# Dilated attention computed on even and odd tokens apart, and the next layer's first weight tile split on GpSimd alone

## The chip, the cores and the metric

The kernel runs on one core of a Trainium2 chip. The metric is device time in microseconds (us) of one execution; less is better. The core's engines are TensorE (PE in the rows, its weight loads PEld), VectorE (DVE), ScalarE (ACT), GpSimd (POOL) and SyncE (SP), which here only issues the DMAs.

## The reference

A decoder trunk of two layers over 256 tokens of width 1024, in float32. Each layer has a gated token mixer (short convolution, RWKV-7 and dilated attention in parallel) and then a mixture of 16 experts, of which each token uses two. The change touches the attention and the seam between the layers. Cut to what matters:

```python
DILATED_GROUPS = ((128, 1), (512, 4), (2048, 16))     # (window, dilation), 8 heads of 64 each
def dilated_attention_branch(z, cos, sin):            # SEQ = 256
    q, k, v = (...)                                   # (B, S, group, head, 64)
    q = apply_partial_rotary(q, cos, sin); k = apply_partial_rotary(k, cos, sin)
    for g, (window, dilation) in enumerate(DILATED_GROUPS):
        # query t attends keys t, t-d, t-2d, ..., t-window
        o, l = dilated_window_attention(q[:, :, g], k[:, :, g], v[:, :, g], window, dilation)
        outs.append(o); lses.append(l)
    wts = jax.nn.softmax(jnp.stack(lses, axis=0), axis=0)
    return sum over g of wts[g] * outs[g]
```

In the groups with dilation 4 and 16 an even token attends only even tokens and an odd token only odd ones.

## The kernel before

**Dense work.** Every dense product of the mixer runs as three fp32r matmuls (`mm3`, lines 405 to 407): input and weight are each split into a rounded part (`hi`) and the rest (`lo`), and hi*hi, hi*lo and lo*hi are added in PSUM. A weight tile of 128x1024 comes by DMA (`load`, line 350, issued by SP), is cast to `wh` on ACT (line 329) and subtracted to `wl` on DVE (line 330), both in `hilo`. `dense_w` makes channels by tokens (weights stationary, 256 tokens moving), `dense_t` tokens by channels (the input `xh`, `xl` stationary, 128 tokens at a time). `dense_t` is used for the attention's values and for the last projection.

**Chains.** The attention and the RWKV waves are generators. After every four contraction steps of dense work `pump` lets each live generator go one `yield` further, so their small matmuls stand between the dense ones in PE's queue. `STAGES` gives the order of the dense work in each layer, `LAG` adds empty steps to the generators. PE takes its queue in order.

**Attention.** For each layer, each half of the heads (`hh`, four heads) and each group `g` there is one generator, 12 in all, 8 of them with `g` = 1 or 2. It rotates q and k (lines 879 to 883); makes the scores in two query blocks, the first against 128 keys, the second against 256 (line 900); adds the mask (904); takes maxima (909); exponentiates (927); transposes the three 128x128 blocks of four heads each (939); copies them (941); multiplies by the values (952), with three blocks again; and merges the group into a running `acc`, with its denominators `den` and shifts `nm` (968 to 978).

**Experts.** In `moe` eight pairs of experts are done in turn: gate and up products (`gu`, line 1444), the activation (`th`, 1457 to 1459), its transpose (`ht`, 1472), the copy `hT` on ACT (1474), the down product (`db`, 1495), its scaled split `yh` on ACT (1499) and `yl` on DVE (1500), and the return to the tokens (`acc`, 1392). Their weights, 100 MB a layer, are used once and come through SP's queue in the order of use.

**The seam.** In the last pair of experts, before the last down matmuls, `split_ahead(nc.gpsimd, 1)` (line 1493) splits the first weight tile of the next layer (`wh`<-`raw`, from `in_wl`): the cast on ACT, the subtraction on POOL. After the last layer there is nothing to split. The order within each engine's queue is set by the scheduler of the framework, not by the text alone.

Of the kernel before, what the change touches and what calls it, by code (L numbers as in the profile page):

```python
# [12 lines left out]
ALU = mybir.AluOpType  # L13
# [4 lines left out]
S = 256  # L18
# [21 lines left out]
def _constants():  # L40

    p = np.arange(128)
    t = np.arange(64)
    out = {}
    out["ident"] = np.eye(128)
    scanm = np.ones((128, 512))
    scanm[:, ::64] = 0.0
    out["scanm"] = scanm
    s = (p % 64)[:, None]
    strict = (s < t[None]).astype(np.float64)  # L50
    incl = (s <= t[None]).astype(np.float64)
# [12 lines left out]
    for window, d in GROUPS:  # L64
        i = (128 + p)[:, None]
        j = np.arange(256)[None]
        ok = (j <= i) & ((i - j) % d == 0) & (i - j <= window)
        am.append(np.where(ok, 0.0, NEG))
    out["amask"] = np.concatenate(am, axis=1)
    out["place"] = np.broadcast_to(t[None] - FAR, (128, 64))  # L70
    inv = np.float32(500000.0) ** (-np.arange(0, 16, 2, dtype=np.float32) / np.float32(16))

    rot = np.zeros((4, 32))
    rot[0::2, :8] = -inv
    rot[1::2, :8] = inv
    out["invf"] = rot.reshape(128, 1)

    out["before"] = np.broadcast_to(np.where(np.tril(np.ones((4, 4)), -1), -1e-37, 0.0).reshape(1, 16), (128, 16))
    mixer = ("scanm", "zmask", "lev", "eye32", "blk", "amask")
# [145 lines left out]
class Net:  # L225
# [98 lines left out]
                                             src[i][:, (2 * pr + cc) * 128:(2 * pr + cc) * 128 + 128], self.c("ident"))  # L324
            yield pr, ps.rearrange("p (c t) -> p c t", c=2)

    def hilo(self, hi, lo, src, eng=None):

        r = self.nc.scalar.copy(hi, src)  # L329
        (eng or self.nc.vector).tensor_tensor(lo, src, hi.bitcast(F32), op=ALU.subtract)  # L330
        return r

# [48 lines left out]
        p = self.tc.tile_pool(name=name, bufs=1)  # L381
        return p, p.__enter__()

    def split_ahead(self, eng=None, n=SPLIT + 1):

        r = []
        i = self.asked
        while i < len(self.plan) and not self.plan[i][2]:
            i += 1
        while len(self.pre) < n and i + len(self.pre) < len(self.plan) and self.plan[i + len(self.pre)][2]:  # L390
            w = self.raw(i + len(self.pre))
            hi = self.t4(w.shape, "wh", F32R)
            lo = self.t4(w.shape, "wl", F32R)
            r.append(self.hilo(hi, lo, w, eng))
            self.pre.append((hi, lo))
        return r

# [27 lines left out]
                    self.pump()  # L425
        return ps

    def dense_t(self, x):

        xh, xl = x  # L430
        ps = [self.bank("dt") for _ in range(2)]
        for hf in range(2):
            wh, wl = self.next_parts()
            for i in range(2):
                t = slice(128 * i, 128 * i + 128)
                for kk in range(4):
# [430 lines left out]

    def attention(self, l, hh, g, q, k, v, st, yc):

        nc = self.nc  # L870
        for _ in range(LAG[l][6]):
            yield
        T = []
        for t, name in ((q, "qT"), (k, "kT")):
            tmp = self.t2([128, 2, S], "rt")
            for o in range(4):

                d, e = slice(32 * o, 32 * o + 32), slice(32 * (o ^ 1), 32 * (o ^ 1) + 32)
                nc.scalar.copy(tmp[d], t[e])
                yield  # L880
            nc.vector.tensor_tensor(tmp, tmp, self.sin.unsqueeze(1).to_broadcast([128, 2, S]), op=ALU.mult)
            nc.vector.tensor_tensor(t, t, self.cos.unsqueeze(1).to_broadcast([128, 2, S]), op=ALU.mult)
            nc.vector.tensor_tensor(t, t, tmp, op=ALU.add)
            T.append(t)
            yield
        for _ in range(LAG[l][7]):
            yield
        qT, kT = T
        s0 = self.t2([128, 2, 2, 128], "s0")
        s1 = self.t4([128, 2, 2, 256], "s1")  # L890
        mx = self.sm([128, 2, 2, 2], "mx")
        am = self.c("amask")
        for qb in range(2):
            nk = 128 * (qb + 1)
            s = (s0, s1)[qb]
            b = [self.bank("sc") for _ in range(2)]
            for hp in range(2):
                for e in range(2):
                    he = slice(64 * e, 64 * e + 64)
                    nc.tensor.matmul(b[e][:, hp * nk:hp * nk + nk], qT[he, hp, qb * 128:qb * 128 + 128], kT[he, hp, 0:nk], start=True, stop=True)  # L900
            yield
            o = g * 256 + 128 - qb * 128
            for e in range(2):
                nc.vector.tensor_tensor(s[:, e, :, :], b[e][:, 0:2 * nk].rearrange("p (h t) -> p h t", h=2),
                                        am[:, o:o + nk].unsqueeze(1).to_broadcast([128, 2, nk]), op=ALU.add)
                if e == 0:
                    yield
            yield
            nc.vector.tensor_reduce(mx[:, qb].rearrange("p hp e -> p e hp"), s, axis=AX.X, op=ALU.max)
        for _ in range(LAG[l][8]):  # L910
            yield
        nm = self.sm([128, 8], "nmx")
        m8 = mx.rearrange("p a b c -> p (a b c)")
        nc.vector.tensor_scalar(nm, m8, -0.125, None, op0=ALU.mult)
        if g:
            acc, den0, nm0 = st[-1]
            nc.vector.tensor_tensor(nm, nm0, nm, op=ALU.min)
            al = self.sm([128, 8], "al")
            nc.vector.tensor_tensor(al, nm, nm0, op=ALU.subtract)
            nc.scalar.activation(al, al, AF.Exp)  # L920
        den = self.sm([128, 8], "den")
        for qb in range(2):
            s = (s0, s1)[qb]
            for hp in range(2):
# [6 lines left out]
        pts = []  # L931
        for qb in range(2):
            s = (s0, s1)[qb]
            for kb in range(qb + 1):
                b = self.bank("pt")
                for hp in range(2):
                    for e in range(2):
                        o = (hp * 2 + e) * 128
                        nc.tensor.transpose(b[:, o:o + 128], s[:, e, hp, kb * 128:kb * 128 + 128], self.c("ident"))
                t = self.t2([128, 4, 128], "PT")  # L940
                nc.scalar.copy(t.rearrange("p a b -> p (a b)"), b)
                pts.append(t)
                yield
# [2 lines left out]
        o = self.bank("o")  # L946
        for qb in range(2):
            for hp in range(2):
                for kb in range(qb + 1):
                    for e in range(2):  # L950
                        h = 2 * hp + e
                        nc.tensor.matmul(o[64 * e:64 * e + 64, hp * 256 + qb * 128:hp * 256 + qb * 128 + 128], v[:, kb, h * 64:h * 64 + 64],
                                         pts[qb + kb][:, h, :], start=(kb == 0), stop=(kb == qb))
        yield
        t = self.t2([128, 2, 256], "oc")
        nc.scalar.copy(t.rearrange("p a b -> p (a b)"), o)
        yield
        o = self.bank("o")
        for qb in range(2):
# [18 lines left out]
            st.append((acc, den, nm))  # L978
        yield
        if g == 2:  # L980
            acc, dn, _ = st[-1]
            rd = self.sm([128, 8], "rd")
            nc.vector.reciprocal(rd, dn)
            nc.vector.tensor_tensor(acc, acc, bc(rd), op=ALU.mult)
# [7 lines left out]
                                        acc[:, i * 4 + cc * 2:i * 4 + cc * 2 + 2, :].rearrange("p h t -> p (h t)"), self.c("ident"))  # L992
            yield
            hi, lo = yc
            bv = b.rearrange("p (c t) -> p c t", c=2)
            self.hilo(hi[0][:, 2 * hh:2 * hh + 2, :], lo[0][:, 2 * hh:2 * hh + 2, :], bv)
            yield

    def mixer(self, l, h, vf):
# [101 lines left out]
        def attn(hh, yc):  # L1101
            st = []
            for g in range(3):
                qkv = []
                for i in range(3):
                    t = self.t2([128, 2, 256], "qkv"[i])
                    if i < 2:
                        nc.scalar.copy(t, two(self.dense_w(x)))
                    else:
                        ps = self.dense_t(x)  # L1110
                        for ii in range(2):
                            nc.scalar.copy(t[:, ii, :], ps[ii][:, 0:256])
                    qkv.append(t)
# [132 lines left out]
    def moe(self, l, u, r, nm, lg):  # L1246
# [171 lines left out]
        for p in range(NE // 2):  # L1418
# [65 lines left out]
            for hf in range(2):  # L1484
                b = self.bank("db")
                for k in range(4):
                    if k % 2 == 0:
                        raw = [self.next_raw() for _ in range(2)]
                    if p == NE // 2 - 1 and hf and k == 2:
                        back(p, 0, ot, yy[0])  # L1490
                        stats(0)
                        self.mo = None
                        self.split_ahead(nc.gpsimd, 1)
                    for e in range(2):
                        nc.tensor.matmul(b[64 * e:64 * e + 64, :], ht[:, k, 64 * e:64 * e + 64], raw[e][:, k % 2, :],  # L1495
                                         start=(k == 0), stop=(k == 3))
# [149 lines left out]
```

## Time and profile before

| what | value |
|---|---|
| time, median of 3 runs | 1609.99 us (1606.95 to 1611.31) |
| time of the profiled execution | 1609.06 us |
| its span, first to last instruction | 1606.9 us |
| PE busy | 1549.3 us (96%) |
| DVE busy | 954.2 us (59%) |
| ACT busy | 694.7 us (43%) |
| POOL busy | 43.4 us (3%) |

The span is 2.2 us shorter than the execution. Roughly, layer 0's mixer takes 0 to 560 us, its experts 560 to 805, layer 1's mixer 805 to 1360 and its experts the rest.

### The profile page before, as it was taken

Reading aid. Unit: us, or ns where it says so; the run is one execution under the profiler, and the core shown is the slowest. Engines: PE = TensorE matmul, PEld = TensorE weight load, DVE = VectorE, ACT = ScalarE, POOL = GpSimd, SP = SyncE. Lnnn points to the kernel's source line nnn. Section 1 sums busy time; section 2 is a strip of 40 time slices with the busy share of each in tenths; the row PEclk is TensorE's granted clock in tenths of the full one; section 3 lists DMA queues with packets and bytes.
Section 4 is the critical chain, followed back from the end, with each engine's and each line's share of the span. In section 5 each row is a group of like instructions: output and inputs, shape, how many; then the busy total and the mean of one; then the engine's idle time right before and its main releaser. Section 6 shows DMA issues by size and latency. Waiting matters only on the chain. (4 is left out here: it accounts for less than half of the span.)

```text
span 1606.9 us, 37830 instructions
## 1 busy us (share of the span) xinstructions
PE 1549.3 (96%) x16202; PEld 1221.5 (76%) x16202; DVE 954.2 (59%) x1788; ACT 694.7 (43%) x1245; POOL 43.4 (3%) x82
## 2 busy tenths in 40 slices
PE   8999999999999999999789999999999999999996
PEld 7999998998999943433289999999889999434332
DVE  7877877968766641112088678778787666311123
ACT  6544666676443321111065466566764433211110
POOL 1000000000000000020000000000000000000200
PEclk9999999999999999999899999999999999999998
DMA  8444443343458959999773444334435489599997
GB/s 343 155 143 134 154 132 100 120 133 100 146 171 302 373 213 409 409 409 409 310 279 123 149 125 133 127 121 132 129 104 152 157 316 372 212 409 409 409 409 277
DMA packets 102701, 369.92 MB, mean 230 GB/s; under 512 B 11392, under 2 KB 12416, under 8 KB 102528
## 3 DMA queue, kind: packets, MB, share of 16 engines
q1 hardware_dynamic: 102528, 367.44, 63.1%
q8 instruction: 129, 2.11, 0.5%
q14 instruction: 44, 0.36, 0.1%
HBM read 363.20 MB, written 4.19 MB: 229 GB/s over the span
## 5 line engine op out<-in xcount | busy, mean ns | idle before, releaser
L405 PE MATMUL dw<-xh,wh 128*128 128x256 f32 x1584 | 469.6, 296 | 0.3
L406 PE MATMUL dw<-xl,wh 128*128 128x256 f32 x1584 | 448.1, 283 | 0.7 <-DVE xl L330 0.7
L407 PE MATMUL dw<-xh,wl 128*128 128x256 f32 x1584 | 447.7, 283 | 0.3 <-DVE wl L330 0.3
L330 DVE TENSOR_TENSOR wl<-raw,wh 128x1024 fp32r<-128x1024 f32 x276 | 331.5, 1214 | 47.3 <-ACT wh L329 19.4
L329 ACT CAST wh<-raw 128x1024 fp32r<-128x1024 f32 x278 | 282.9, 1045 | 98.0 <-DVE wl L330 53.2
L405 PEld LDWEIGHTS dw<-xh,wh 128*128 128x128 f32 x1584 | 301.2, 190 | 16.1 <-issue 4.7
L406 PEld LDWEIGHTS dw<-xl,wh 128*128 128x128 f32 x1584 | 302.1, 191 | 2.3 <-DVE xl L330 1.2
L407 PEld LDWEIGHTS dw<-xh,wl 128*128 128x128 f32 x1584 | 301.3, 190 | 0.9 <-DVE wl L330 0.5
L1444 PE MATMUL gu<-raw,xg 128*64 128x512 f32 x600 | 150.8, 597 | 2.0 <-PE ot L1381 1.6
L1500 DVE SCALAR_TENSOR_TENSOR yl<-db,cs,yh 128x512 fp32r<-128x512 f32 x32 | 24.0, 751 | 152.4 <-ACT yh L1499 150.6
L1444 PE MATMUL gu<-mo,xg 128*64 128x512 f32 x424 | 113.1, 597 | 0.8 <-DMA mo<-in_we 0.6
L1444 PEld LDWEIGHTS gu<-raw,xg 128*64 128x64 f32 x600 | 45.4, 137 | 82.0 <-issue 74.5
L1495 PE MATMUL db<-raw,hT 128*64 128x512 f32 x344 | 88.9, 612 | 11.2 <-ACT hT L1474 11.2
L1444 PEld LDWEIGHTS gu<-mo,xg 128*64 128x64 f32 x424 | 33.6, 136 | 57.7 <-issue 47.9
L1495 PEld LDWEIGHTS db<-raw,hT 128*64 128x64 f32 x344 | 27.1, 140 | 61.5 <-issue 46.7
L1499 ACT ACTIVATE yh<-db,cs 128x512 fp32r<-128x512 f32 x32 | 22.0, 688 | 110.2 <-PE db L1495 110.2
L1457 ACT ACTIVATE th<-gu 128x512 f32<-128x512 f32 x16 | 9.6, 598 | 133.7 <-PE gu L1444 133.7
L1474 ACT COPY hT<-ht 128x512 f32<-128x512 f32 x16 | 9.4, 585 | 115.4 <-PE ht L1472 115.4
L405 PE MATMUL dt<-wh,xh 128*128 128x256 f32 x192 | 57.5, 300 | 0.0
L1459 DVE TENSOR_TENSOR th<-th,gu 128x512 f32<-128x512 f32 x16 | 11.0, 687 | 77.3 <-PE gu L1444 77.3
L406 PE MATMUL dt<-wl,xh 128*128 128x256 f32 x192 | 55.0, 286 | 0.0
L407 PE MATMUL dt<-wh,xl 128*128 128x256 f32 x192 | 54.1, 282 | 0.0
(378 smaller groups left out, 2738.7 us busy)
## 6 DMA issues: line engine op xcount, KB each, us to landing
raw<-in_wm SPq DMA_DIRECT2D x272, 512.0 KB, 3.7
raw<-in_we SPq DMA_DIRECT2D x236, 512.0 KB, 10.2
mo<-in_we SPq DMA_DIRECT2D x148, 512.0 KB, 10.2
lo<-in_lo SPq DMA_DIRECT2D x8, 512.0 KB, 4.5
ng<-in_norms SPq DMA_DIRECT2D x5, 512.0 KB, 10.2
nb<-in_norms SPq DMA_DIRECT2D x5, 512.0 KB, 10.2
raw<-in_wl SPq DMA_DIRECT2D x4, 512.0 KB, 8.6
hsave<-h SPq DMA_DIRECT2D x4, 512.0 KB, 4.8
```

Source lines behind the costliest of these rows:

```text
L329: r = self.nc.scalar.copy(hi, src)
L330: (eng or self.nc.vector).tensor_tensor(lo, src, hi.bitcast(F32), op=ALU.subtract)
L405: nc.tensor.matmul(out, lh, rh, start=first, stop=False)
L406: nc.tensor.matmul(out, lh, rl, start=False, stop=False)
L407: nc.tensor.matmul(out, ll, rh, start=False, stop=last)
L1444: nc.tensor.matmul(b[64 * e:64 * e + 64, :], xg[k // 4][:, k % 4, p % 2, 64 * e:64 * e + 64], raw[e][:, k % 2, :], start=(k == 0), stop=(k ...
L1457: nc.scalar.activation(t, gu[0], AF.Tanh, scale=0.5)
L1459: V.tensor_tensor(t, t, gu[1], op=ALU.mult)
L1474: nc.scalar.copy(ht.rearrange("p a b -> p (a b)"), b)
L1495: nc.tensor.matmul(b[64 * e:64 * e + 64, :], ht[:, k, 64 * e:64 * e + 64], raw[e][:, k % 2, :], start=(k == 0), stop=(k == 3))
L1499: last = nc.scalar.activation(yh, b, AF.Copy, scale=w)
L1500: V.scalar_tensor_tensor(yl, b, w, yh.bitcast(F32), op0=ALU.mult, op1=ALU.subtract)
```

## The change

Two edits in one.

In `split_ahead` at the seam, the cast is handed to GpSimd too: both halves of that one tile's split are now in POOL's queue.

In the attention, groups 1 and 2 keep their tokens sorted into even ones and odd ones. q and k are copied out of PSUM in that order (the copy reads every second element), the cosine and sine tables are read with a step of two, and the values come out of `dense_t` with `step` 2, which takes every second token of `xh` and `xl` as the stationary operand. Each query block then meets only the 128 keys of its own parity: scores of 128x128 in both blocks, two blocks of transposes and copies and products with the values where there were three. The mask tables shrink (1856 to 1600 columns in `cstm`). Group 0 stays as it was, but its result is brought into the sorted order: the copy `oc` reads PSUM with a step of two, and `den` and `nm`, now together in `pk`, are permuted by four small matmuls with every second column of the identity as stationary operand, and a copy on DVE. The last split of the attention's output writes with a step of two, back into token order. A generator with `g` > 0 has one `yield` less.

```diff
-    def hilo(self, hi, lo, src, eng=None):
-        r = self.nc.scalar.copy(hi, src)
+    def hilo(self, hi, lo, src, eng=None, copy=None):
+        r = (copy or self.nc.scalar.copy)(hi, src)
...
-    def dense_t(self, x):
+    def dense_t(self, x, step=1):
...
-                t = slice(128 * i, 128 * i + 128)
+                t = slice(128 * i, 128 * i + 128) if step == 1 else slice(i, S, 2)
...
-            nk = 128 * (qb + 1)
+            k0, nk = (128 * qb, 128) if g else (0, 128 * (qb + 1))
...
-                    nc.tensor.matmul(b[e][:, hp * nk:hp * nk + nk], qT[he, hp, qb * 128:qb * 128 + 128], kT[he, hp, 0:nk], start=True, stop=True)
+                    nc.tensor.matmul(b[e][:, hp * nk:hp * nk + nk], qT[he, hp, qb * 128:qb * 128 + 128], kT[he, hp, k0:k0 + nk], start=True, stop=True)
...
-            for kb in range(qb + 1):
+            for kb in range(1 if g else qb + 1):
...
-                for kb in range(qb + 1):
+                for kb in range(qb if g else 0, qb + 1):
...
+        if not g:
+            b = self.bank("pk")
+            for qb in range(2):
+                for i in range(2):
+                    nc.tensor.matmul(b[64 * qb:64 * qb + 64, i * 8:i * 8 + 8], self.c("ident").rearrange("p (t q) -> p q t", q=2)[:, i, :],
+                                     pk[:, :, qb * 4:qb * 4 + 4], start=True, stop=True)
...
-                    if i < 2:
+                    if i < 2 and g:
+                        nc.scalar.copy(t.rearrange("p c (q t) -> p c q t", q=2), self.dense_w(x).rearrange("p (c t q) -> p c q t", c=2, q=2))
+                    elif i < 2:
                         nc.scalar.copy(t, two(self.dense_w(x)))
                     else:
-                        ps = self.dense_t(x)
+                        ps = self.dense_t(x, 1 + (g > 0))
...
-                        self.split_ahead(nc.gpsimd, 1)
+                        self.split_ahead(nc.gpsimd, 1, nc.gpsimd.tensor_copy)
```

What this does to the queues, at three places. First ACT's queue at the seam, before:

```order
L1457 ACTIVATE th_9275<-gu_9241 128x512
L329 CAST wh_9330<-raw_9299 128x1024
L1474 COPY hT_9288<-ht_9283 128x512
L1499 ACTIVATE yh_9305<-db_9294,cs_9139 128x512
L1499 ACTIVATE yh_9338<-db_9309,cs_9139 128x512
```

and now:

```order
L1483 ACTIVATE th_9243<-gu_9209 128x512
L1500 COPY hT_9256<-ht_9251 128x512
L1525 ACTIVATE yh_9273<-db_9262,cs_9107 128x512
L1525 ACTIVATE yh_9306<-db_9277,cs_9107 128x512
L1446 TENSOR_LOAD cnti_8052
```

The cast of the next layer's tile stood ahead of `hT`, the operand of the last pair's down product, and is gone from ACT.

POOL's queue at the same place, before:

```order
L517 MEMSET P_10033 128x8
L1145 MEMSET tcv_10123 128x2x2
L330 TENSOR_TENSOR wl_9331<-raw_9299,wh_9330 128x1024
L1420 TENSOR_LOAD cnti_8084
L1509 COMPARE_AND_BRANCH
```

and now:

```order
L519 MEMSET P_10001 128x8
L1171 MEMSET tcv_10091 128x2x2
L331 CAST wh_9298<-raw_9267 128x1024
L332 TENSOR_TENSOR wl_9299<-raw_9267,wh_9298 128x1024
L1446 TENSOR_LOAD cnti_8052
L1535 COMPARE_AND_BRANCH
```

The cast stands ahead of the subtraction; the two memsets ahead and the branch behind are the same.

PE's queue in layer 0's mixer, where group 1's product with the values (`o`<-`PT`,`v`) meets group 2's first scores (`sc`), before:

```order
L952 MATMUL o_3692<-PT_3550,v_2699 64x128 x4
L952 MATMUL o_3692<-PT_3588,v_2699 64x128 x2
L952 MATMUL o_3692<-PT_3631,v_2699 64x128 x2
L952 MATMUL o_3692<-PT_3588,v_2699 64x128 x2
L952 MATMUL o_3692<-PT_3631,v_2699 64x128 x2
L900 MATMUL sc_3708<-k_2996,q_2848 128x128
L900 MATMUL sc_3709<-k_2996,q_2848 128x128
```

and now:

```order
L763 MATMUL ub_3645<-G_3630,TF_2551 64x64 x4
L963 MATMUL o_3652<-PT_3556,v_2699 64x128 x4
L963 MATMUL o_3652<-PT_3594,v_2699 64x128 x4
L409 MATMUL dw_3602<-xh_133,wl_3454 128x256
```

Twelve matmuls have become eight, and they stand one pump earlier, behind a RWKV step (`ub`) and ahead of dense work.

## Rows read from the trace of the kernel before

**Rows 1.** Windows of both mixers: stretch, its length, busy time by engine, clock, DMA

```profile
40.00:300.00 260.00, 258.53 (x3422) 241.34 (x3422) 204.04 (x387) 154.25 (x289) 4.91 (x20) 1.00 0.42 134
300.00:520.00 220.00, 217.43 (x3058) 203.86 (x3057) 158.06 (x270) 116.62 (x214) 2.03 (x6) 1.00 0.50 164
...
830.00:1100.00 270.00, 268.73 (x3505) 251.71 (x3505) 214.88 (x393) 162.78 (x303) 6.18 (x24) 1.00 0.43 138
1100.00:1300.00 200.00, 196.45 (x2875) 183.22 (x2874) 152.85 (x274) 115.46 (x212) 1.84 (x6) 0.99 0.45 139
```

**Rows 2.** Timeline of PE around a score block of 256 keys: start, length, instruction

```profile
204.44 0.28 PE L406 MATMUL dw<-xl,wh 128*128 128x256 f32 x1
204.56 0.28 PE L407 MATMUL dw<-xh,wl 128*128 128x256 f32 x1
204.77 1.14 PE L900 MATMUL sc<-k,q 64*128 64x256 f32 x8
205.83 0.39 PE L405 MATMUL dw<-xh,wh 128*128 128x256 f32 x1
```

**Rows 3.** Timeline of PE: value products, then a score block of 128 keys

```profile
224.27 1.53 PE L952 MATMUL o<-PT,v 128*64 128x128 f32 x24
225.73 0.71 PE L900 MATMUL sc<-k,q 64*128 64x128 f32 x8
226.37 0.38 PE L405 MATMUL dt<-wh,xh 128*128 128x256 f32 x1
```

**Rows 4.** Timeline of PE around four transposes

```profile
217.55 0.60 PE L939 MATMUL pt<-ident,s 128*128 128x128 f32 x4
217.90 0.36 PE L405 MATMUL dt<-wh,xh 128*128 128x256 f32 x1
```

**Rows 5.** Timeline of PE around very narrow matmuls (layer 1)

```profile
856.41 0.63 PE L594 MATMUL nb<-cstm,sq 128*64 128x2 f32 x16
856.97 0.38 PE L405 MATMUL dw<-xh,wh 128*128 128x256 f32 x1
```

**Rows 6.** Weight loads of `dense_t`, 150 to 400 us: busy time, mean ns

```profile
L405 PEld LDWEIGHTS dt<-wh,xh 128*128 128x128 f32 x96 | 18.3, 191 | 1.3 <-issue 0.5
```

**Rows 7.** Timeline of ACT at the seam of the layers, with idle time ahead

```profile
790.54 1.04 ACT L329 CAST wh<-raw 128x1024 fp32r<-128x1024 f32 x1 [19.10 <-SPq L1509]
791.49 0.58 ACT L1474 COPY hT<-ht 128x512 f32<-128x512 f32 x1
...
803.14 0.69 ACT L1499 ACTIVATE yh<-db,cs 128x512 fp32r<-128x512 f32 x1 [4.04 <-PE db L1495]
```

**Rows 8.** Window of the seam while PE stands, columns as in rows 1

```profile
783.50:792.10 8.60, 0.00 (x0) 0.00 (x0) 0.00 (x0) 1.53 (x2) 0.44 (x1) 0.71 1.03 407
```

**Rows 9.** Timeline of DVE: the last pair's activation in layer 0, in layer 1

```profile
781.02 0.69 DVE L1459 TENSOR_TENSOR th<-th,gu 128x512 f32<-128x512 f32 x1 [8.86 <-PE gu L1444]
...
1582.02 0.69 DVE L1459 TENSOR_TENSOR th<-th,gu 128x512 f32<-128x512 f32 x1 [8.16 <-PE gu L1444]
```

**Rows 10.** Timeline of ACT at the end of layer 1, the last pair

```profile
1593.02 0.69 ACT L1499 ACTIVATE yh<-db,cs 128x512 fp32r<-128x512 f32 x1 [4.21 <-PE db L1495]
```

**Rows 11.** Timeline of SP: the last ten expert weights, layer 0, layer 1

```profile
767.54 11.85 SPq L350 DMA_DIRECT2D raw<-in_we  x10
...
1568.53 11.87 SPq L350 DMA_DIRECT2D raw<-in_we  x10
```

**Rows 12.** Timeline of PE: layer 1's first dense matmul

```profile
813.83 0.76 PE L405 MATMUL dw<-xh,wh 128*128 128x256 f32 x1
```

**Rows 13.** POOL: groups by line with mean ns, then its timeline at 707 us

```profile
L1253 POOL TENSOR_SCALAR h<-h,lny,nm 128x1024 f32<-128x1024 f32 x2 | 2.4, 1195 | 341.3 <-DVE lg L1242 172.1 <-DMA raw<-in_we 169.3
...
707.54 4.69 POOL L1455 TENSOR_TENSOR h<-h,ng 128x1024 f32<-128x1024 f32 x2 [139.83 <-DMA ng<-in_norms]
```

**Rows 14.** Timeline of DVE while POOL works

```profile
709.88 0.75 DVE L1500 SCALAR_TENSOR_TENSOR yl<-db,cs,yh 128x512 fp32r<-128x512 f32 x1 [2.68 <-ACT yh L1499]
```

**Rows 15.** ACT's copies of q out of PSUM, by line and shape

```profile
L1108 ACT COPY q<-dw 128x512 f32<-128x512 f32 x12 | 7.0, 583 | 26.7 <-PE dw L407 26.5 <-ACT wh L329 0.3
```

More of the change, by code (lines that the diff above doesn't have):

```diff
@@ L64, in _constants @@
     for window, d in GROUPS:
-        i = (128 + p)[:, None]
-        j = np.arange(256)[None]
-        ok = (j <= i) & ((i - j) % d == 0) & (i - j <= window)
+        n = 1 + (d % 2 == 0)
+        i = (256 // n - 128 + p)[:, None]
+        j = np.arange(256 // n)[None]
+        ok = (j <= i) & (n * (i - j) % d == 0) & (n * (i - j) <= window)
         am.append(np.where(ok, 0.0, NEG))
@@ L382, in open_pool, with split_ahead @@
         return p, p.__enter__()
-    def split_ahead(self, eng=None, n=SPLIT + 1):
+    def split_ahead(self, eng=None, n=SPLIT + 1, copy=None):
         r = []
@@ L393, in split_ahead @@
             lo = self.t4(w.shape, "wl", F32R)
-            r.append(self.hilo(hi, lo, w, eng))
+            r.append(self.hilo(hi, lo, w, eng, copy))
             self.pre.append((hi, lo))
@@ L880, in attention @@
                 yield
-            nc.vector.tensor_tensor(tmp, tmp, self.sin.unsqueeze(1).to_broadcast([128, 2, S]), op=ALU.mult)
-            nc.vector.tensor_tensor(t, t, self.cos.unsqueeze(1).to_broadcast([128, 2, S]), op=ALU.mult)
+            for a, b in ((tmp, self.sin), (t, self.cos)):
+                if g:
+                    a = a.rearrange("p c (q t) -> p c q t", q=2)
+                    b = b.rearrange("p (t q) -> p q t", q=2).unsqueeze(1).to_broadcast([128, 2, 2, 128])
+                else:
+                    b = b.unsqueeze(1).to_broadcast([128, 2, S])
+                nc.vector.tensor_tensor(a, a, b, op=ALU.mult)
             nc.vector.tensor_tensor(t, t, tmp, op=ALU.add)
@@ L889, in attention @@
         s0 = self.t2([128, 2, 2, 128], "s0")
-        s1 = self.t4([128, 2, 2, 256], "s1")
+        s1 = self.t4([128, 2, 2, 128] if g else [128, 2, 2, 256], "s1")
         mx = self.sm([128, 2, 2, 2], "mx")
@@ L899, in attention @@
                     he = slice(64 * e, 64 * e + 64)
-                    nc.tensor.matmul(b[e][:, hp * nk:hp * nk + nk], qT[he, hp, qb * 128:qb * 128 + 128], kT[he, hp, 0:nk], start=True, stop=True)
+                    nc.tensor.matmul(b[e][:, hp * nk:hp * nk + nk], qT[he, hp, qb * 128:qb * 128 + 128], kT[he, hp, k0:k0 + nk], start=True, stop=True)
             yield
-            o = g * 256 + 128 - qb * 128
+            o = 128 + g * 128 if g else 128 - qb * 128
             for e in range(2):
@@ L911, in attention @@
             yield
-        nm = self.sm([128, 8], "nmx")
+        if g:
+            nm, den = self.sm([128, 8], "nmx"), self.sm([128, 8], "den")
+        else:
+            pk = self.sm([128, 2, 8], "pk")
+            den, nm = pk[:, 0, :], pk[:, 1, :]
         m8 = mx.rearrange("p a b c -> p (a b c)")
@@ L915, in attention @@
         if g:
-            acc, den0, nm0 = st[-1]
+            acc, den0, nm0 = st[g - 1]
             nc.vector.tensor_tensor(nm, nm0, nm, op=ALU.min)
@@ L920, in attention @@
             nc.scalar.activation(al, al, AF.Exp)
-        den = self.sm([128, 8], "den")
         for qb in range(2):
@@ L952, in attention @@
                         nc.tensor.matmul(o[64 * e:64 * e + 64, hp * 256 + qb * 128:hp * 256 + qb * 128 + 128], v[:, kb, h * 64:h * 64 + 64],
-                                         pts[qb + kb][:, h, :], start=(kb == 0), stop=(kb == qb))
+                                         pts[qb if g else qb + kb][:, h, :], start=(g > 0 or kb == 0), stop=(kb == qb))
+        if not g:
[4 more added lines that the diff above has]
+                                     pk[:, :, qb * 4:qb * 4 + 4], start=True, stop=True)
+            pk = self.sm([128, 2, 2, 4], "pk")
+            nc.vector.tensor_copy(pk, b[:, 0:16].rearrange("p (i n h) -> p n i h", i=2, n=2))
+            den, nm = (pk[:, i].rearrange("p a b -> p (a b)") for i in range(2))
         yield
         t = self.t2([128, 2, 256], "oc")
-        nc.scalar.copy(t.rearrange("p a b -> p (a b)"), o)
+        if g:
+            nc.scalar.copy(t.rearrange("p a b -> p (a b)"), o)
+        else:
+            nc.scalar.copy(t.rearrange("p a (q t) -> p a q t", q=2), o.rearrange("p (a t q) -> p a q t", a=2, q=2))
         yield
@@ L980, in attention @@
         if g == 2:
-            acc, dn, _ = st[-1]
+            acc, dn, _ = st[g]
             rd = self.sm([128, 8], "rd")
@@ L994, in attention @@
             hi, lo = yc
-            bv = b.rearrange("p (c t) -> p c t", c=2)
-            self.hilo(hi[0][:, 2 * hh:2 * hh + 2, :], lo[0][:, 2 * hh:2 * hh + 2, :], bv)
+            bv = b.rearrange("p (c q t) -> p c q t", c=2, q=2)
+            self.hilo(*(a[0][:, 2 * hh:2 * hh + 2, :].rearrange("p c (t q) -> p c q t", q=2) for a in (hi, lo)), bv)
             yield
```

## The prediction

> **What bounds the kernel now.** I read the stages first, then PE's timeline inside the attention, then the seam between the layers. In the mixers PE is the bound: over the four windows that hold the attention PE is busy for 941.1 of 950 us, while DVE is busy 77% and ACT 58% of the time and DMA uses half of its share or less [rows 1]. The reader should see that PE stands for only 8.9 us in those 950, so an instruction that leaves PE's queue there gives back its time, as long as no new wait appears. The dense matmuls follow each other every 0.12 us, although each is shown 0.28 long, because they overlap [rows 2]; so prices on PE are taken from one start to the next, not from durations.
>
> At the seam it is different. PE does nothing at all from 783.5 to 792.1 us, while DMA runs at full rate (407 GB/s) [rows 8]. ACT waits 19.10 us for the next layer's first tile, starts its cast at 790.54, and only then does `hT`, the operand of the last pair's down product, at 791.49 [rows 7]. The row names SP's branch as the releaser, but that instruction moves no data into `raw`; the tile comes by DMA behind the expert weights, so I read the wait as one for the tile. `hT` was wanted some 8 us earlier. The end of layer 1 shows the same last pair without such a cast, and serves as the model.
>
> **The seam, worked out.** In layer 0 the last activation starts on DVE at 781.02 and the last `yh` on ACT at 803.14 [rows 7, 9], 22.1 us later. In layer 1 the same two stand at 1582.02 and 1593.02 [rows 9, 10], 11.0 us apart. The weights do not explain the difference: SP finishes issuing the last ten expert tiles at 779.39 in layer 0 and at 1580.40 in layer 1 [rows 11], 1.63 and 1.62 us ahead of the activation. So without the cast ahead of `hT`, layer 0 should be done 11.1 us earlier. [...] Everything behind the last `yh` is one chain up to layer 1's first dense matmul at 813.83 [rows 12], which then stands at 802.7.
>
> What the edit adds is a cast on POOL. The trace has no such cast. Below it is bounded by POOL's one-input operation on the same shape, 1.20 us, above by its two-input one, 2.35 us each [rows 13]; I take 2 us, nearer to the upper, since a cast here also changes the type. The tile lands at about 790.5, so with both operations at the upper bound the split is over by 795.2, against 802.7 when the first product wants it: 7.5 us of cover; were that gone, the two would cost at most 4.7 us. Queued behind it on POOL are a read of the token count, a branch and a memset whose tile is used after the first dense products; no other engine waits there. DVE's `yl` falls into the same stretch as POOL's work. A `yl` at 709.88, inside a POOL operation that runs from 707.54 to 712.23, took 0.75 us [rows 13, 14], so I charge nothing for sharing.
>
> **The attention, worked out.** Only groups 1 and 2 change: 2 layers x 2 halves x 2 groups = 8 generators. Per generator PE loses:
> - scores of 256 keys become scores of 128: 1.06 us (204.77 to 205.83) [rows 2] become 0.64 (225.73 to 226.37) [rows 3]; 8 x 0.42 = 3.4 us;
> - one block of four transposes, 0.35 us from its start to the next start [rows 4]; 8 x 0.35 = 2.8 us;
> - 24 records of the value product become 16: 1.46 us for 24 [rows 3], so 0.061 each; 8 x 8 x 0.061 = 3.9 us.
>
> Together 10.1 us. Each switch between dense and small work costs some 0.09 us ahead (0.21 from 204.56 to 204.77 where 0.12 is usual) [rows 2] and about as much behind; by the order of the queue the change merges or removes only a few such breaks, worth 0 (none) to 1.5 us (one in each generator, 8 x 0.19); I take 0.75, between them. Added are four permutations for group 0, 8 records each. Nearest below are the two-column matmuls, 0.56 us for 16 or 0.035 each [rows 5], above the 0.061 of the value product: 1.1 to 2.0 us in all; I take 1.5, between them. Net 10.1 + 0.75 - 1.5 = 9.4 us.
>
> **Edits that I cost at nothing.** The 16 copies of q and k that read PSUM with a step of two are on ACT, 0.58 us each now [rows 15]; were each twice as long, that would be 9.3 us over both mixers on an engine that is idle for over 40% of them [rows 1]. The generators wait for these copies, but PE has dense work meanwhile. The four `oc` copies, the table reads and the split written with a step lie on ACT and DVE too, and DVE and ACT lose more than they gain (half of the masking, of the maxima and of the exponentials of the second block, a third of the transposed blocks' copies). If that cover failed, PE would wait, which is the third rival. Group 1 now waits for the permuted `nm` of group 0, which comes later than the old one, but behind the value product of a generator that started twelve pumps earlier.
>
> **The step in the stationary operand.** The values' `dense_t` now loads `xh` and `xl` with every second token: 8 generators x 48 = 384 loads. A load takes 191 ns when contiguous, under matmuls that start every 120 ns [rows 2, 6], so loads are close to being a bound themselves. No row shows one with gaps. Bounds: nothing, or half the rate, so that 0.12 becomes 0.24 and 384 x 0.12 = 46 us are lost. I take nothing, because the nearest row is the load of the same shape and tile. [...]
>
> **Sum.** 1609.06 of the profiled execution (the span and the 2.2 us around it) - 11.1 - 9.4 = 1588.6. The median of the runs shown lies 0.9 above that execution, so 1589.5 us. About 0.3% (4.8 us) is what a measurement of this kernel can tell from no change.
>
> **Rivals.**
> - *The stepped loads are slow* (the other side). Place: PE, the 8 `dense_t` calls that make the changed groups' values. It decides at 20.5 / 384 = 53 ns a matmul: above that the change loses. At the full 120 ns: 1589.5 + 46 = 1635.5. For it speaks that PEld is nearly as busy as PE [rows 1]; against it only that 4-byte elements two apart are still close together. Chance 0.09.
> - *The seam does not shorten*, because the last expert weights come late and PE waits for them instead. 1589.5 + 11.1 = 1600.6. Against it stands layer 1, where the same weights are issued at the same distance [rows 9 to 11]. Chance 0.05.
> - *PE's saving turns into waits.* With less small work between pumps the generators' steps on DVE and ACT come due sooner, DVE is at 77%, and PE takes its queue in order, so one late operand stops the dense work too. If all is lost: 1589.5 + 9.4 = 1598.9; half, 1594.2. For it: the order of work was tuned by `LAG` to the old steps. Against: PE stood only 8.9 us in 950 [rows 1], and DVE and ACT have less to do. Chance of losing more than half: 0.11.
> - *Neither does anything*: 1610; chance 0.02.
>
> **How the numbers follow.** My forecast has 0.73. Its own range takes the bounds: 0.75 more from the breaks, 0.4 from the permutations and a quarter of PE's 8.9 us of standing less gives 1586; half of the attention's saving lost gives 1594.2. To leave out no more than 2 in 10 the range goes up over most of the third rival, to 1598. Faster by over 0.3% (below 1605.2) needs half of the sum and holds in the forecast, the second and third rivals and a small part of the first: 0.91. Within 0.3%: 0.03. Slower: 0.06, nearly all of it the first rival.
>
> **What would show it.** Right: at the seam ACT does `hT` within 2 us of the activation, POOL shows a cast of 1 to 2.4 us, PE has no gap of several us before the down product, and the activation and the last `yh` stand 11 us apart; dense matmuls of the stepped `dense_t` still start every 0.12 us; score blocks of `g` > 0 take 0.64 us; PE's standing time in the mixers stays near 9 us. Wrong: weight loads longer than 191 ns or starts further apart in the values' products; the gap before the down product filled by a wait for `in_we`; more PE waits for `s`, `PT` or `oc`; layer 1's first dense product waiting for `wh` or `wl` from POOL.

## The result and the profile after

| what | before | after |
|---|---|---|
| median | 1610.65 us (4 runs, 1606.95 to 1611.53) | 1587.09 us (4 runs, 1586.12 to 1588.90) |
| time of the profiled execution | 1609.06 us | 1586.12 us |

The ratio is 0.9859, 95% interval [0.9841, 0.9878]: the change gains 23.6 us, where 20.5 were forecast. The page of the changed kernel: its span, and the busy time and instructions of each engine.

```profile
span 1584.3 us, 37699 instructions
...
PE 1536.6 (97%) x16138; PEld 1214.3 (77%) x16138; DVE 946.6 (60%) x1792; ACT 685.8 (43%) x1236; POOL 44.3 (3%) x83
```

**The seam.** Timelines of ACT, DVE and POOL at the last pair of layer 0, in that order (start, length, instruction, idle time ahead and its releaser):

```profile
775.26 0.59 ACT L1500 COPY hT<-ht 128x512 f32<-128x512 f32 x1 [10.21 <-PE ht L1498]
779.79 0.69 ACT L1525 ACTIVATE yh<-db,cs 128x512 fp32r<-128x512 f32 x1 [3.94 <-PE db L1521]
784.52 0.69 ACT L1525 ACTIVATE yh<-db,cs 128x512 fp32r<-128x512 f32 x1 [4.05 <-PE db L1521]
...
773.68 0.69 DVE L1485 TENSOR_TENSOR th<-th,gu 128x512 f32<-128x512 f32 x1 [7.92 <-PE gu L1470]
...
785.24 0.75 DVE L1526 SCALAR_TENSOR_TENSOR yl<-db,cs,yh 128x512 fp32r<-128x512 f32 x1 [1.79 <-ACTq L1535]
...
783.33 1.04 POOL L331 CAST wh<-raw 128x1024 fp32r<-128x1024 f32 x1 [12.01 <-SPq L1535]
784.45 2.37 POOL L332 TENSOR_TENSOR wl<-raw,wh 128x1024 fp32r<-128x1024 f32 x1
```

`hT` starts 1.58 us after the activation `th` (775.26 - 773.68) and waits for nothing but its transpose; before, it stood behind a 19.10 us wait [rows 7]. Activation to last `yh` is 10.84 us, as in layer 1 before (11.00) [rows 9, 10]; in layer 0 before it was 22.1. The wait for the tile is still there, on POOL, where it holds up nothing but the subtraction: the tile is cast at 783.33, later than the first `yh`. The split is over at 786.8, and PE wants it 8 us later. PE around the down product, and the first dense matmul of layer 1, with the same down product before as the last line:

```profile
774.62 0.60 PE L1498 MATMUL ht<-ident,th 128*128 128x128 f32 x4
...
776.09 5.37 PE L1521 MATMUL db<-raw,hT 128*64 128x512 f32 x24
...
795.01 0.47 PE L407 MATMUL dw<-xh,wh 128*128 128x256 f32 x1
```

```profile
792.12 7.96 PE L1495 MATMUL db<-raw,hT 128*64 128x512 f32 x24 [8.65 <-ACT hT L1474]
```

No wait is shown ahead of any of the three after. Before, PE stood 8.65 us for `hT`, and the 24 products behind that stand took 7.96 us instead of 5.37, at a granted clock of 0.50 from 792.1 to 796 us: 8.65 + 2.59 = 11.2, nearly the whole gain of the seam. The window of the last pair (columns as in rows 1) shows PE busy for 10.95 of 11.00 us at a clock of 1.00, where it stood for 8.6 us [rows 8]:

```profile
773.50:784.50 11.00, 10.95 (x49) 4.73 (x48) 2.74 (x4) 1.27 (x2) 1.09 (x2) 1.00 1.03 408
```

**The attention.** PE's timeline around a group 0 product with the values, its permutation (`pk`) and the scores behind it; then products with the values and scores of a group with `g` > 0:

```profile
224.82 1.53 PE L963 MATMUL o<-PT,v 128*64 128x128 f32 x24
226.18 0.42 PE L970 MATMUL pk<-pk,ident 128*64 128x8 f32 x8
226.53 0.72 PE L908 MATMUL sc<-k,q 64*128 64x128 f32 x8
...
252.49 1.09 PE L963 MATMUL o<-PT,v 128*64 128x128 f32 x16
253.51 0.28 PE L409 MATMUL dw<-xh,wl 128*128 128x256 f32 x1
...
255.03 0.71 PE L908 MATMUL sc<-k,q 64*128 64x128 f32 x8
255.68 0.39 PE L407 MATMUL dw<-xh,wh 128*128 128x256 f32 x1
```

From start to next start, 16 products with the values take 1.02 us and eight scores 0.65, about as reckoned from [rows 3] (0.98 and 0.64). The next scores start at 226.53, so a permutation takes 0.35. The four windows of the mixers, moved with the work of layer 1 (columns as in rows 1):

```profile
40.00:300.00 260.00, 259.60 (x3435) 243.32 (x3434) 204.42 (x392) 156.12 (x291) 4.90 (x20) 1.00 0.43 135
300.00:520.00 220.00, 217.96 (x3065) 205.29 (x3065) 159.61 (x275) 116.45 (x213) 2.01 (x6) 1.00 0.53 176
815.00:1085.00 270.00, 267.63 (x3551) 251.10 (x3553) 214.35 (x398) 161.38 (x303) 6.13 (x24) 1.00 0.43 134
1085.00:1285.00 200.00, 196.28 (x2848) 184.32 (x2835) 147.57 (x266) 110.60 (x206) 1.79 (x6) 0.99 0.47 149
```

PE is busy 941.5 of 950 us: its standing time, 8.5 us, is about what it was. But it has moved. PE's waits between 830 and 1300 us, in layer 1 (what PE waited for; us in total, times, longest):

```profile
PE ub L763 <- ACT G L758: 2.6, 2, 2.2
PE mw L687 <- DVE TT L695: 1.6, 2, 1.0
PE o L985 <- ACT oc L980: 0.7, 1, 0.7
PE m L687 <- issue: 0.5, 1, 0.5
PE sb L772 <- DVE UV L765: 0.4, 1, 0.4
PE dw L409 <- DVE wl L332: 0.3, 1, 0.3
```

The first wait was there before, but short; in the kernel before, between the same times, the long one was for `UV`:

```profile
PE sb L770 <- DVE UV L763: 1.5, 1, 1.5
...
PE ub L761 <- ACT G L756: 0.6, 2, 0.4
```

What is new is the single wait of 2.2 us for `G`. ACT's row for it; then the window behind it, and the window behind the wait for `UV` in the kernel before:

```profile
1148.03 0.27 ACT L758 COPY G<-gb 128x128 f32<-128x128 f32 x1 [2.26 <-DVE k L891]
```

```profile
1150.00:1155.00 5.00, 5.00 (x49) 4.46 (x46) 1.13 (x3) 0.93 (x3) 0.00 (x0) 0.68 0.03 11
```

```profile
1169.00:1174.00 5.00, 5.00 (x54) 4.52 (x56) 1.89 (x5) 0.74 (x2) 0.00 (x0) 0.66 0.37 108
```

The RWKV step's copy `G` waits 2.26 us for DVE's rotation of the attention's `k` (line 891), which does not compute anything that `G` reads. `G` takes its tile from the pool `t2`, and the rotation takes its temporaries from the same pool, so I read the wait as one for a buffer. Behind it PE works without a gap (5.00 of 5.00 us) at a granted clock of 0.68 on average: 0.50 from 1150 to 1153 us, 0.89 in the next us and 1.00 in the one after. That is not new either: behind the 1.5 us wait for `UV` the kernel before shows 0.66.

### The profile page after: what moved, and what is told of

It is laid out like the page before. It is cut to its first block, busy times and chain, and to the rows that moved or that the text cites. A ratio compares the mean times of both kernels' runs of the same rounds, so it can differ in the third digit from the quotient of the medians.

```text
span 1584.3 us, 37699 instructions
## 1 busy us (share of the span) xinstructions
PE 1536.6 (97%) x16138; PEld 1214.3 (77%) x16138; DVE 946.6 (60%) x1792; ACT 685.8 (43%) x1236; POOL 44.3 (3%) x83
## 5 line engine op out<-in xcount | busy, mean ns | idle before, releaser
L331 ACT CAST wh<-raw 128x1024 fp32r<-128x1024 f32 (+1 forms) x277 | 282.1, 1045 | 75.0 <-DVE wl L332 52.1
```

Source lines behind the costliest of these rows:

```text
L331: r = (copy or self.nc.scalar.copy)(hi, src)
```

## The experiments

Each time is a median, and each ratio stands against runs of the kernel before on the same chip, whose medians were 1609.7 to 1610.7 us.

**One edit at a time.** `attn_only` undoes the seam's edit in the kernel after (the first pair of lines), `seam_only` makes it alone in the kernel before (the second, with the parameter `copy` that it needs).

```diff
-                        self.split_ahead(nc.gpsimd, 1, nc.gpsimd.tensor_copy)
+                        self.split_ahead(nc.gpsimd, 1)
...
-                        self.split_ahead(nc.gpsimd, 1)
+                        self.split_ahead(nc.gpsimd, 1, nc.gpsimd.tensor_copy)
```

> The attention edit without the seam edit: ACT does the cast of the next layer's first tile again. Theory A (two independent gains: PE loses some 10 to 11 us of attention work, the seam gives 11 to 12 by the order of ACT's queue alone): 1599 to 1601 us, 10 to 12 below before; PE stands 8 to 9 us ahead of the last pair's down product and its activation and last yh are 22 us apart again. Rival B (the attention edit is worth less by itself, and part of its gain was seen only because the seam had become short): 1603 or more.

> The seam edit without the attention edit. Theory A: 11 to 12 us below before, so 1599 to 1600; activation and last yh of layer 0 are 11 us apart, the mixers' spans are unchanged. Rival B: the seam is worth less without the attention edit because the expert weights then land later relative to PE: 1603 or more, and PE waits for in_we ahead of the down product.

Measured: `attn_only` 1597.48 us, ratio 0.9926 [0.9912, 0.9940], so the attention alone gains 12.2 us; `seam_only` 1598.93 us, ratio 0.9931 [0.9917, 0.9944], so the seam alone gains 10.8. Together 23.0, against 23.6 for both: they add up. `attn_only` came out 1.5 us below the range of theory A. ACT in `attn_only` shows the old picture at the seam, the cast ahead of `hT` and the last `yh` 22.1 us behind the activation (773.23 to 795.33):

```profile
782.77 1.04 ACT L331 CAST wh<-raw 128x1024 fp32r<-128x1024 f32 x1 [18.32 <-SPq L1535]
783.72 0.58 ACT L1500 COPY hT<-ht 128x512 f32<-128x512 f32 x1
...
795.33 0.69 ACT L1525 ACTIVATE yh<-db,cs 128x512 fp32r<-128x512 f32 x1 [4.05 <-PE db L1521]
```

**Is it the queue or the engine?** Two other places for the first tile's split: the cast on DVE (`seam_dve`, the first pair of lines), and no split ahead at all (`no_split`, where the line is gone).

```diff
-                        self.split_ahead(nc.gpsimd, 1, nc.gpsimd.tensor_copy)
+                        self.split_ahead(nc.gpsimd, 1, nc.vector.tensor_copy)
...
-                        self.split_ahead(nc.gpsimd, 1, nc.gpsimd.tensor_copy)
```

> The changed kernel with the cast of the next layer's first tile on DVE instead of GpSimd. In DVE's queue it stands ahead of the last pair's activation th. Theory by queue order (what was dear before was not ACT's time, but that a wait for the tile stood ahead of the pair's own work in an in-order queue): DVE waits for the tile to about 783, th starts some 10 us later than the 773.68 of the changed kernel, and the time is 1596 to 1599 us, as with the cast on ACT. Rival (it was ACT that was short there, or ACT's cast that was slow): 1587 +- 1.5 us.

> The changed kernel without any split at the seam; the tile is split by ACT and DVE in the ordinary way when layer 1 begins. Theory J (the seam's gain is the place in ACT's queue alone, and who splits the tile hardly matters): 0 to 2.5 us slower than the changed kernel, the most being one cast and one subtraction (1.05 + 1.22 us) on the path ahead of the first dense product. Rival K (the early split on POOL is itself worth a good part of the seam's 11 us): 5 us slower or more.

`seam_dve`: 1599.60 us, ratio 0.9941 [0.9927, 0.9955], 12.4 above the changed kernel, a little past the range given. DVE's timeline there, and PE's transpose and down product:

```profile
782.98 0.69 DVE L331 CAST wh<-raw 128x1024 fp32r<-128x1024 f32 x1 [17.77 <-SPq L1535]
783.59 0.68 DVE L1485 TENSOR_TENSOR th<-th,gu 128x512 f32<-128x512 f32 x1
...
784.32 1.11 PE L1498 MATMUL ht<-ident,th 128*128 128x128 f32 x4 [9.81 <-DVE th L1485]
787.07 6.65 PE L1521 MATMUL db<-raw,hT 128*64 128x512 f32 x24
```

DVE's cast is the shortest of the three (0.69 us) and DVE had nothing else to do, yet `th` starts at 783.59 instead of 773.68. Of those 9.9 us the cast is 0.6 (782.98 to 783.59), and the rest is the wait for the tile. Most of what is left of the 12.4 is PE's slower work behind its stand, at a granted clock of 0.50 from 784.3 to 789.5 us: the same 24 down products take 6.65 us where they took 5.37. So it was the place in an in-order queue, whichever engine's, that was dear.

`no_split`: 1591.81 us, ratio 0.9882 [0.9867, 0.9897], 4.6 above the changed kernel and between the two expectations. PE and ACT at layer 1's start:

```profile
797.62 0.39 PE L407 MATMUL dw<-xh,wh 128*128 128x256 f32 x1 [2.23 <-ACT wh L331]
...
798.88 0.58 PE L409 MATMUL dw<-xh,wl 128*128 128x256 f32 x1 [0.68 <-DVE wl L332]
```

```profile
796.52 1.05 ACT L331 CAST wh<-raw 128x1024 fp32r<-128x1024 f32 x1
```

ACT takes the tile only after its copies and casts of the input, though in the changed kernel the tile was there by 783. PE waits 2.23 and 0.68 us for the two halves, and the layer's first stretch (first dense matmul to first score) is 2.0 us longer. Its first dense matmuls run at a granted clock of 0.50, where the changed kernel shows 1.00 from 795.2 to 801.5 us:

```profile
798.00:804.50 6.50, 5.82 (x28) 5.62 (x27) 5.43 (x6) 3.44 (x5) 0.00 (x0) 0.50 1.03 412
```

So most of the seam's gain is to keep the tile's wait out of the pair's queues, and a part, 4.6 us, is to do the split ahead at all: about half of that is the wait for it, the rest, by my estimate from these rows, mostly the clock behind that wait.

**The step of the stationary operand.** In the stepped `dense_t` the stationary operand takes every 4th, or every 8th, element instead of every 2nd (the diff is that of `step4`; `step8` has 8 for the last 4). Both read other tokens and channels than they should, so these kernels' values mean nothing; the loads and matmuls are as many as before.

```diff
-                    self.mm3(ps[i][:, 0:256], xh[hf][:, kk, t], xl[hf][:, kk, t], wh[:, kk, :], wl[:, kk, :],
+                    a, c = xh[hf][:, kk, t], xl[hf][:, kk, t]
+                    if step > 1:
+                        w = slice(128 * kk + i, 128 * kk + i + 509, 4)
+                        a, c = (z[hf].rearrange("p k t -> p (k t)")[:, w] for z in x)
+                    self.mm3(ps[i][:, 0:256], a, c, wh[:, kk, :], wl[:, kk, :],
...
```

> The changed kernel, but the stepped loads of the values' product take every fourth element (16 bytes apart) of the same tiles instead of every second, so the values are wrong ones; all else is the same. [...] Rival D (a step in the stationary operand costs nothing at any of these widths): 1587, within 3 us, and loads stay near 195 ns.

> As the run with every fourth element, but every eighth (32 bytes apart); again wrong values. [...] Rival D: 1587, within 3 us. A third way, a price that grows with the distance: clearly above the run with every fourth.

`step4` took 1633.31 us (ratio 1.0146 [1.0131, 1.0162]), `step8` 1633.41 (1.0147 [1.0132, 1.0163]): 46.2 and 46.3 above the changed kernel, and slower than before. Weight loads of `dense_t` over the whole run, after, `step4` and `step8` (a third of these 192 is group 0's, without a step):

```profile
L408 PEld LDWEIGHTS dt<-wl,xh 128*128 128x128 f32 x192 | 37.2, 194 | 1.0 <-issue 1.0
```

```profile
L408 PEld LDWEIGHTS dt<-wl,xh 128*128 128x128 f32 x192 | 54.5, 284 | 1.0 <-issue 1.0
```

```profile
L408 PEld LDWEIGHTS dt<-wl,xh 128*128 128x128 f32 x192 | 55.6, 289 | 1.0 <-issue 1.0
```

PE's timeline in a stepped `dense_t`, after and in `step4`:

```profile
193.52 0.28 PE L409 MATMUL dt<-wh,xl 128*128 128x256 f32 x1
193.64 0.28 PE L407 MATMUL dt<-wh,xh 128*128 128x256 f32 x1
```

```profile
193.45 0.40 PE L407 MATMUL dt<-wh,xh 128*128 128x256 f32 x1
193.68 0.40 PE L408 MATMUL dt<-wl,xh 128*128 128x256 f32 x1
```

Starts are 0.12 us apart with a step of 2 and 0.23 to 0.24 with 4; 384 x 0.12 = 46.1, the whole difference. Every second float cost nothing that the starts of the matmuls show (the loads take 194 ns against 191 [rows 6]), every fourth doubles the distance of the matmuls, and going from every fourth to every eighth adds 0.1 us to the time, less than the runs scatter, and 5 ns to the mean load. So rival D fell at both, and a price that grows with the distance did too. What in the load sets the price is not shown, nor what a step of three would cost.

**The new stand, and the yield.** Five kernels: the changed one again; one that keeps the old number of yields; one with a buffer more in the pool `t2` (room for it comes from a scan mask of half the width, so the scan is done in two halves); that one again; and both edits. The first pair of lines below is the yield's, the others are the buffer's.

```diff
-        for _ in range(LAG[l][10]):
+        for _ in range(LAG[l][10] + (g > 0)):
...
-N4, N2, NG, NP, NZ, NSM, NSS, AHEAD, AHEAD_M, AHEAD_E, SPLIT, NM, NT = 31, 19, 6, 2, 1, 12, 2, 5, 22, 41, 2, 15, 16
+N4, N2, NG, NP, NZ, NSM, NSS, AHEAD, AHEAD_M, AHEAD_E, SPLIT, NM, NT = 31, 20, 6, 2, 1, 12, 2, 5, 22, 41, 2, 15, 16
...
-    scanm = np.ones((128, 512))
+    scanm = np.ones((128, 256))
```

> The changed kernel once more, on the same chip as the other three of this set, as their yardstick. All theories: 1586 to 1589. If the run with two tiles fewer waits is to be told from it, its stand of 2.2 us ahead of a RWKV product (ub) in layer 1 must be there again.

> The changed kernel with the step that generators of groups 1 and 2 lost put back (one empty step ahead of the value product), so that they go on in the old rhythm. Theory E (part of the gain of 12 us of the attention edit, 9.4 forecast, comes from the shorter generators, whose work meets other waits): 1 to 4 us slower than the changed kernel. Rival F (the gain is PE work alone, the step count does not matter): within 1 us of it.

> The changed kernel with 20 instead of 19 buffers for the mixer's working tiles (t2), paid for by a scan mask of 256 columns and two scans of 256 in place of one of 512. Theory G (the stand of 2.2 us in layer 1, where the copy G on ACT waits for DVE's k, is G's wait for a buffer that k's rotation still holds): that stand goes, 1584 to 1586, 1 to 3 us faster than the changed kernel. Rival H (G waits for its place in ACT's queue or for PE): the stand stays and the time is the same within 1 us.

> The same kernel as n2_20, once more, as yardstick for the run with both mends on the same chip: 1581.5 to 1584 us.

> The changed kernel with both mends: one more buffer of the t2 pool, and the groups with g > 0 keep the yield that the change took from them. Theory L (the two gains are of different places: the buffer takes away the stand of 2.2 us in layer 1, the yield moves small work in layer 0, where the first score to the attention's projection got 1.8 us shorter): they add up, 1587.1 - 4.6 - 1.9 = about 1580.6 us. Theory M (both only shift the same generators by a pump, and there is one gain to be had): no better than the buffer alone, 1582 to 1584.

| kernel | median, us | ratio to before, 95% | layer 0, first score to projection | layer 1, the same |
|---|---|---|---|---|
| after_again | 1587.24 | 0.9859 [0.9844, 0.9874] | 229.04 | 263.00 |
| keep_yield | 1585.26 | 0.9845 [0.9831, 0.9858] | 227.23 | 262.78 |
| n2_20 | 1582.65 | 0.9830 [0.9817, 0.9844] | 229.16 | 258.06 |
| n2_20_again | 1583.09 | 0.9831 [0.9817, 0.9844] | 229.13 | 258.04 |
| n2_keep | 1581.76 | 0.9823 [0.9809, 0.9836] | 227.39 | 257.96 |

The last two columns are us on PE from the first score to the first dense product of the attention's output; 235.46 and 267.41 in the kernel before, 229.01 and 262.97 in the changed one. With one more buffer the wait for `G` is gone from PE's list between 830 and 1300 us, and so are those for `oc` and `UV`:

```profile
PE mw L688 <- DVE TT L696: 1.6, 2, 1.0
PE dw L409 <- DVE wl L332: 0.3, 1, 0.3
```

That takes 4.9 us from layer 1's stretch and nothing from layer 0's, where the scan is done in two halves as well, and 4.6 (4.2 in the second run) from the time: more than the 1 to 3 of theory G. More went than the stand for `G`: the slow stretch behind it is gone too (the clock is 1.00 from 1140 to 1165 us in `n2_20`). The trace of `attn_only` has the stand but not the slow stretch:

```profile
1160.50:1165.50 5.00, 5.00 (x64) 4.61 (x60) 1.28 (x4) 1.49 (x4) 0.00 (x0) 1.00 0.06 25
```

Its layer 1 stretch takes 261.5 us, against 263.0 in the changed kernel and 258.1 with the buffer, so of the 4.9 us, by an estimate from these three, about 1.5 are the clock and 3.4 the waits. (The waits listed fall from 6.1 to 1.9 us, in the second run, with the same stretch, only to 2.8.) So the stand was one for a buffer of `t2`. Both theories of `keep_yield` fell: with the old yields the kernel is 2.0 us faster by the medians (the intervals overlap, but its slowest run, 1586.32, is below the fastest of the changed kernel on that chip, 1586.75), 1.8 of them in layer 0, where PE switches from dense to small work 72 times instead of 74. Both together gain 1.3 us over the buffer alone, between the two theories and within the scatter of the runs; the traces show the two gains side by side in the two layers (227.39 and 257.96), so I take them as separate, which the times alone do not show. `n2_keep` is the best kernel measured, 28.3 us under the one before. Whether the kernel before would have gained from that buffer as well was not tried; its waits for `UV`, `oc` and `G` in layer 1 are of the kind that left with it.

**The kernel before, once more.**

> The kernel before, unchanged, profiled once more, for layer 0's experts. From their first gate product to their last they took 203.0 us in its trace and 203.1 in that of the seam edit alone, but 201.2 to 201.6 in every trace with the attention edit; layer 1's take 201.2 to 202.7 in whichever kernel. If that belongs to the kernel (another start of the stream of weights): 202.9 to 203.3 again. If it is chance of the execution: anything from 201.2 to 202.7 is as likely. The seam's landmarks again: activation to last yh 22 us.

It took 1613.23 us in its single run. From the start of the first gate product to the start of the very last, layer 0's experts took 203.4 us there and 203.9 in the first trace of the same kernel, 204.5 in that of `seam_only`, and 202.5 to 202.9 in every trace with the attention's edit; layer 1's took 202.5 to 203.5 in whichever kernel. The figures of the expectation are starts of rows that hold four to six of the last products, so they do not compare with each other or with these. Two traces of one kernel lie 0.5 us apart, against 1.4 between before and after; yet the three traces with the old attention lie above all the others. So this decides neither for chance nor for the kernel, and I don't count the 1.4 us as a gain whose cause is known. DMA is full there in any case (1.01 of its share, 401 GB/s, from 590 to 770 us before). Activation to last `yh` took 22.4 us (22.1 in the first trace).

## Why the prediction was right

**The seam, forecast 11.1.** Right in mechanism and size: 10.8 by `seam_only`, and in the traces 11.3 from the activation to the last `yh` (22.12 before, 10.84 after) and 11.5 from the start of the last gate product to layer 1's first dense matmul (33.44 before, 21.96 after). Every sign named in advance for the seam is there. What bounded POOL's cost was too high: the cast takes 1.04 us, below even the 1.20 of the lower bound and as long as on ACT [rows 7], not 2. It cost nothing either way, since the cover is 8 us. DVE's `yl` at 785.24 runs inside POOL's subtraction and takes 0.75 us, as read from [rows 13, 14].

**The attention, forecast 9.4.** Right in mechanism, too small: 10.9 in the changed kernel's trace (6.45 in layer 0 and 4.44 in layer 1, from the first score to the projection), 12.2 by the time of `attn_only`. The terms, as sums over the traces of PE's time from each start to the next, between first score and projection, both layers:

| term | forecast | traces, before to after |
|---|---|---|
| scores | -3.4 | 21.06 to 17.65: -3.4 |
| transposes (and waits inside and just behind them) | -2.8 | 18.50 to 13.38: -5.1 |
| products with the values (and the return `o`) | -3.9 | 22.47 to 18.82: -3.65 |
| permutations | +1.5 | +1.26 |
| breaks and waits | -0.75 | near 0 beyond those inside the rows above |

The transposes were mis-sized. I priced a block of four at the 0.35 us of one that was among the cheapest [rows 4]. In layer 1, where each of the 18 blocks before and of the 14 now stands in one piece, a block takes 0.45 us on average before and 0.43 after, and the four fewer gave 2.05 us instead of 1.4. In layer 0 they gave 3.06 us instead of 1.4: there the 18 blocks stood in 23 pieces, now 14 in 14, and PE itself waited inside them, four times, 0.7 us in all, a wait that is not on the list after:

```profile
278.22 0.33 PE L939 MATMUL pt<-ident,s 128*128 128x128 f32 x1 [0.16 <-ACT s L927]
```

How much of the excess of 2.3 us is breaks and how much the price of a block is not measured apart. The four terms make up the whole 10.9; what is left nearly cancels: the RWKV step `sb` no longer waits for `UV` in layer 0 (1.6 us before, not on the list after) and less in layer 1, while layer 1 got the long stand for `G`.

The stretches of `attn_only` lost 6.43 and 5.91 us; the 1.5 more in layer 1 is the slow stretch that its trace does not have and that the kernel before, the changed one and its second trace all have. That trace is of the fastest of its five runs (1595.89 against the median of 1597.48), so how much of the 12.2 us is clock is not known; the 10.9 compares two traces that both have the slow stretch.

In the two profiled executions the spans differ by 22.6 us (1606.9 and 1584.3): 11.5 at the seam, 10.9 in the attention's stretches, 1.4 in layer 0's experts, less 1.0 by which the stretch from layer 1's first dense matmul to its first score got longer (169.8 to 170.8). The last two were not forecast and have no known cause.

**The stepped load, taken as nothing.** Right, and the bound from above was the true price at a step of 4: 46.2 us measured against the 46 of the rival. A step of 4 would have turned this change into a loss of some 23 us. The rival had the right size, but at that wider step: with every second float the starts stayed 0.12 us apart. That it would be free was an estimate from the contiguous load of the same shape and tile, and why it was free no run shows.

**PE's saving turns into waits.** In sum it did not: the standing time was 8.9 us and came out as 8.5, because old waits went and a new one came. In layer 1 the listed waits rose from 4.8 to 6.1 us, with the stand of 2.2 us among them, and in layer 0 they fell. The 4.2 to 4.6 us that the buffer gives back are therefore mostly not a price of the change: the slow stretch, and a stand of 1.5 us ahead of it, were in the kernel before.

**Edits at nothing.** They held. ACT's copies of q and k that read PSUM with a step take as long as those of group 0 without one; ACT groups by line and shape, after:

```profile
L1132 ACT COPY q<-dw 128x512 f32<-128x512 f32 x8 | 4.7, 583 | 19.6 <-PE dw L409 19.3 <-ACT wh L331 0.3
...
L1134 ACT COPY q<-dw 128x512 f32<-128x512 f32 x4 | 2.3, 581 | 0.8 <-PE dw L409 0.8
```

What stays open: which switches of PE's queue the kept yield removes in layer 0, why the same stand at `G` was followed by a slow clock in the changed kernel's traces but not in that of `attn_only`, and what made layer 0's experts 1.4 us shorter.

## What to carry to other kernels

In these runs an instruction that waited for a transfer held up what stood behind it in its engine's queue (on ACT `hT`, for which PE stood 8.65 us, on DVE `th`, 9.9 us late); so put such a one on the engine whose queue holds nothing urgent, even a slower one, as long as it is done before its result is wanted (here 8 us before), and not on the fastest one. When small work is cut from a full PE, price the pieces as they stand in the queue and not as one block, then look for the stands that are left: here they came of a pool of buffers one short, and one more gave 4.2 to 4.6 us, though PE's waits in sum had not grown. Before a stationary operand is read with a step, measure its matmuls' starts at that step: every second float was free here, every fourth cost 0.12 us a matmul.

## What the hardware showed unexpectedly

- The cast of 128x1024 floats to fp32r takes 1.04 us on POOL, 1.04 on ACT and 0.69 on DVE, while POOL's subtraction of the same shape takes 2.37.
- A weight load from every 4th float takes 284 ns on average over a group of which a third is not stepped, so by estimate about (284 - 191 / 3) x 3 / 2 = 330 ns where it is; from every 8th float hardly more (289 on average).
- A stand of 2.2 us in a PE that was otherwise busy throughout was followed by 5 us at a mean granted clock of 0.68 in the changed kernel, and by 5 us at 1.00 in `attn_only`, with the same order of work. In the kernel before, a stand of 1.5 us was followed by 5 us at 0.66. The difference in the stretch's length is 1.5 us.
